# Memory attention begins its first query slices inside the layer norm ahead of it, and the SP queue issues the MoE parameter loads

## The chip, the cores and the metric

One core of a Trainium2 chip runs the whole program once. The metric is device time in microseconds (us) of one execution. 0.3% of it is 5.1 us.

## The reference, cut to what matters

The program is two blocks over 256 tokens of width 1024. The second has two layers, and each runs a mixer, a memory attention and a mixture of experts, with a layer norm after every one:

```python
def layer_norm(x, g, b):
    xf = x.astype(jnp.float32)
    mu = jnp.mean(xf, axis=-1, keepdims=True)
    xc = xf - mu
    var = jnp.mean(xc * xc, axis=-1, keepdims=True)
    y = xc * lax.rsqrt(var + LN_EPS) * g + b
...
def memory_cross_attention(x, mem_k, mem_v, w_q, w_out):
    q = (x @ w_q).reshape(bsz, seq, MEM_HEADS, MEM_HEAD_DIM) * (MEM_HEAD_DIM ** -0.5)
    s = jnp.einsum('bshd,bmhd->bhsm', q, mem_k)
    p = jax.nn.softmax(s, axis=-1)
    o = jnp.einsum('bhsm,bmhd->bshd', p, mem_v).reshape(bsz, seq, MEM_HEADS * MEM_HEAD_DIM)
    return o @ w_out
...
    for i in range(DEPTH):                       # DEPTH is 2
        mix = differential_attention(...) if i == 0 else dsa_sparse_mla(...)
        h = layer_norm(alpha * h + mix, ln_g[i, 0], ln_b[i, 0])
        h = layer_norm(alpha * h + memory_cross_attention(h, ...), ln_g[i, 1], ln_b[i, 1])
        h = layer_norm(alpha * h + hierarchical_moe(h, ...), ln_g[i, 2], ln_b[i, 2])
```

w_q is 1024 by 1024: four heads of 256 columns.

## The kernel before, in words

All matmuls with weights from memory are done in split precision. `split` (L183) makes of a 128x1024 slab a rounded high part `wh` (a cast on ACT, L201, type fp32r) and the rest `wl` (a subtraction, L202, on DVE unless the caller names another engine), and a product is three matmuls: high by high, low by high, high by low. `mm3` (L225 to L227) issues the three for each of the 8 blocks of the contraction; `mm3s` (L240, L241, L243) issues the products with the high part of x first, then the 8 with the low part.

**The end of a mixer.** `diff` (layer 0) and `dsa` (layer 1) end with `nat` (its matmuls are at L225 to L227 with 512 moving columns): the output projection, which leaves two accumulators for each of the two token tiles t = 0, 1 (128 tokens each). Then they call the first layer norm of their layer, called norm 1 here.

**Norm 1** (`layer_norm`, L360 on) runs tile by tile. For each t: DVE adds the mixer to the residual with a row sum (L366, twice 512 columns), makes the mean (L368), ACT squares (L372, twice), DVE subtracts the mean and multiplies by the gain (L375, twice), makes the variance (L376, L377), POOL raises it to the power -1/2 (L378), and DVE scales and shifts (L384, twice). Then PE transposes the tile in 8 blocks (L260), ACT rounds the transpose to `xh` (L263, twice) and DVE takes the rest `xl` (L266, twice). The `xl` of tile 0 are held back (`defer`) until the variance of tile 1 has been sent to POOL.

**Memory attention** (`memattn`, L1432). A queue object (`MoeQueue`) holds the order in which SP loads weight slabs into a ring of buffers (tile name `mw`), and `stream` gives a function that waits for the next slab. Eight q slices of 128 columns (two for a head) are each cast, split and multiplied with all 256 tokens (`proj_T` and `mm3s`: 24 matmuls of 256 columns a slice). After the slices of head 0, PE computes its scores (L1459); slices 2 and 3 (head 1) stand ahead of them. The loop `for n in range(6)` staggers q, softmax (`soft`) and values (`pv`) of the four heads. Then `nat` runs with the output weights, and the second norm of the layer.

**MoE parameters** (`moe_prep`, L1510 on). Nine small loads for the router (`wr` in four pieces, `br` in two, `ust`, `iota`, `first4`) are issued by ACT (L1519 to L1532). `moe_prep` is called between the mixer and `memattn`; ACT has its rows between the casts of the mixer's output weights and the squares of norm 1. They are first read in `route`, at the end of the memory attention's second norm.

The order of instructions on each engine is set by the order of the code and by `tc.issue_after(ins)`, which holds what is written inside it behind the instruction `ins`.

Of the kernel before, what the change touches and what calls it, by code (L numbers as in the profile page):

```python
# [14 lines left out]
AF = mybir.ActivationFunctionType  # L15
ALU = mybir.AluOpType
# [113 lines left out]
class Block:  # L130
# [49 lines left out]
        self.loaded = self.nc.sync.dma_start(v, ap).ins  # L180
        return v

    def split(self, raw, lo_eng=None, pool=None, spare=False):  # L183
        nc = self.nc
        n = int(np.prod(raw.shape[1:]))
        r = []
        if spare == "nrm":
            sp = [self.gp.tile([128, 1024], F32R, tag="nrm", name="sp") for _ in range(2)]
        elif spare:
            sp = self.xp.tile([128, 2, 1024], F32R, tag="xl", name="sp")  # L190
            sp = [sp[:, u] for u in range(2)]
# [12 lines left out]

    def rows(self, ap, lo_eng=None, pool=None):
# [152 lines left out]
    def layer_norm(self, x, mix, li, n, xh=None, xl=None, x32=None, alpha=ALPHA, after=None, fold=1):  # L358
        nc = self.nc
        gb, bb = self.bcast(self.i["ln_g_2"][li, n]), self.bcast(self.i["ln_b_2"][li, n])  # L360
        defer = []
        for t in range(2):
            st = self.small(8, "ln")
            for hf in range(2):
                sl = slice(hf * 512, hf * 512 + 512)
                nc.vector.scalar_tensor_tensor(x[:, t, sl], x[:, t, sl], alpha, mix[t][hf], op0=ALU.mult, op1=ALU.add,  # L366
                                               accum_out=st[:, hf:hf + 1])
            nc.vector.tensor_scalar(st[:, 2:3], st[:, 0:1], st[:, 1:2], -1.0 / D, op0=ALU.add, op1=ALU.mult)  # L368
            sc = self.gp.tile([128, 1024], F32, tag="nrm", name="nrm")
            for hf in range(2):  # L370
                sl = slice(hf * 512, hf * 512 + 512)
                nc.scalar.activation(mix[t][hf], x[:, t, sl], AF.Square, bias=st[:, 2:3], accum_out=st[:, 6 + hf:7 + hf])  # L372
            for hf in range(2):
                sl = slice(hf * 512, hf * 512 + 512)
                nc.vector.scalar_tensor_tensor(sc[:, sl], x[:, t, sl], st[:, 2:3], gb[:, sl], op0=ALU.add, op1=ALU.mult)  # L375
            nc.vector.tensor_scalar(st[:, 3:4], st[:, 6:7], st[:, 7:8], 1.0 / D, op0=ALU.add, op1=ALU.mult)  # L376
            nc.vector.tensor_scalar(st[:, 4:5], st[:, 3:4], 1e-5, None, op0=ALU.add)  # L377
            nc.gpsimd.tensor_tensor(st[:, 5:6], st[:, 4:5], self.mhalf, op=ALU.pow)  # L378
            for f in defer:
                f()  # L380
            for hf in range(2):
                sl = slice(hf * 512, hf * 512 + 512)
                a, b = (v[:, sl].rearrange("p (q k) -> p k q", k=fold) for v in (sc, bb))
                nc.vector.scalar_tensor_tensor(x[:, t, sl].rearrange("p (k q) -> p k q", k=fold), a, st[:, 5:6], b,  # L384
                                               op0=ALU.mult, op1=ALU.add)
# [909 lines left out]
    def diff(self, h):  # L1295
        nc, i, tc = self.nc, self.i, self.tc
# [63 lines left out]
                        nc.vector.scalar_tensor_tensor(o[1][:, j - 1], p[:, 0:256], self.subg, o[0][:, j - 1],  # L1360
                                                       op0=ALU.mult, op1=ALU.subtract)
        acc = self.nat(o, self.rows(wo), lag=4, spare=True)
        x = self.xT()
        self.layer_norm(h, acc, 0, 0, *x)
        return x

    def diff_rope(self, da, t, acc, tag):
        q = self.gp.tile([128, 1024], F32, tag=tag, name="roped")
# [60 lines left out]
            nc.vector.tensor_scalar(on[:, t], po[:, t * 128:t * 128 + 128], s2[:, 4 + t:5 + t], None, op0=ALU.mult)  # L1429
        return on  # L1430

    def memattn(self, h, x, li, after=None):  # L1432
        nc, i, tc = self.nc, self.i, self.tc
        vec, mm = nc.vector, nc.tensor.matmul
        with ExitStack() as es:
            o = self.xT()
            qs, sms = {}, {}
            mq = self.moe_queue
            qcols = mq.stream(2, lambda w, j: self.split(w[:, :, j * 128:j * 128 + 128]))
# [68 lines left out]
    def moe_prep(self, li, es):  # L1508
# [6 lines left out]
            return mc.tile(shape, dt, name=name)  # L1515

        wr = one([128, 8, 20], "wr")
        for c in range(2):
            nc.scalar.dma_start(wr[:, 4 * c:4 * c + 4, 0:4], i["moe_w_group_2"][li, c * 512:c * 512 + 512].rearrange("(p k) g -> p k g", k=4),  # L1519
                                allow_slow_non_contiguous=True)  # L1520
        for c in range(2):
            nc.scalar.dma_start(wr[:, 4 * c:4 * c + 4, 4:20], i["moe_w_expert_2"][li, c * 512:c * 512 + 512].rearrange("(p k) g -> p k g", k=4),
                                allow_slow_non_contiguous=True)
        br = one([128, 20], "br")
        nc.scalar.dma_start(br[:, 0:4], i["moe_b_group_2"][li].partition_broadcast(128))
        nc.scalar.dma_start(br[:, 4:20], i["moe_b_expert_2"][li].partition_broadcast(128))
        ust = one([128, 128], "ust")
        nc.scalar.dma_start(ust, i["ustrict"])
        iota = one([128, 64], "iota")
        nc.scalar.dma_start(iota, i["iota64"])  # L1530
        first4 = one([128, 4], "first4")
        nc.scalar.dma_start(first4, i["first4"])  # L1532
# [60 lines left out]
        r["route"] = route  # L1593
        return r

    def moe(self, h, x32, r, li, last=False):
# [166 lines left out]
    def dsa(self, h, x):  # L1763
# [35 lines left out]
        for t in range(2):  # L1799
# [9 lines left out]
            p = self.ps()  # L1809
# [160 lines left out]
        x = self.xT()  # L1970
        self.layer_norm(h, acc, 1, 0, *x)
        return x


def build(tc, ins, out, start=0, stop=99, hin=None):
    with ExitStack() as es:
# [16 lines left out]
        if stop > 4:  # L1993
# [7 lines left out]
            for li in range(2):  # L2001
                i = b.i
                mem = run((5, 8)[li])
                q = MoeQueue(b.nc, i["xa_w_q_2"][li] if mem else None, i["xa_w_out_2"][li], i["moe_w_gate_2"][li], i["moe_w_up_2"][li], i["moe_w_down_2"][li])
                b.moe_queue = q
                b.extra = 2
                with ExitStack() as ms:
                    early = (4, 6)[li]
                    q.add(ms.enter_context(tc.tile_pool(name="ma", bufs=early, side="right")), early)
                    if run((4, 7)[li]):  # L2010
                        with b.weights(2048, 5 - li, 4):
                            x = (b.dsa(h, x or b.test_x(h)) if li else b.diff(h))
                    for n in (5, 9 - early):
                        q.add(ms.enter_context(tc.tile_pool(name="mw", bufs=n, side="right")), n)
                    r = b.moe_prep(li, ms)
                    q.fetch()
                    if mem:
                        with b.weights(2048, 0, 4):
                            x = b.memattn(h, x or b.test_x(h), li, r["route"] if run((6, 9)[li]) else None)
                    if run((6, 9)[li]):  # L2020
                        if x is None:
                            x = b.test_x32(h)
# [28 lines left out]
```

## Time and profile before

| what | value |
|---|---|
| runs | 1700.69, 1703.74, 1705.14 us; median 1703.74 us |
| the profiled execution | 1703.31 us, span from first to last instruction 1701.2 us, mean granted clock 0.971 |
| busy over the span | PE 1588.7 us (93%), PE weight loads 1157.7, DVE 840.1 (49%), ACT 655.8 (39%), POOL 95.8 (6%) |
| norm 1 of layer 0 | from the last matmul of `nat`, 948.69, to the first scores of head 0, 973.88 us |
| norm 1 of layer 1 | from 1379.84 to 1401.86 us |

How to read it: the page gives for each engine its busy time and the share of the span. A timeline row gives start and length, engine, line, operation, output and inputs by name, shapes, the count of instructions gathered into the row, and in brackets the idle time of the engine before it with what released it. PEld is the weight load of a matmul, which runs beside the matmul before. Rows of PE and PEld say f32 for fp32r too. A length is from start to the modelled end, and ends overlap the next start, so distances are taken from start to start. PEclk is the granted clock of TensorE as a share of full speed.

### The profile page before, as it was taken

The numbers are of one execution on the slowest core, as the hardware profiler recorded it, in microseconds if no ns is written. First come the engines' busy times: TensorE is split into PE (matmuls) and PEld (weight loads), VectorE is DVE, ScalarE is ACT, GpSimd is POOL, SyncE is SP. The second block draws the span as 40 slices with busy tenths as digits, with TensorE's granted clock in tenths as the row PEclk, the third lists the DMA queues.
The fourth block names the chain that finished last, engine by engine and source line by source line (L and its number), as shares of the span: only waits on it lengthen the run. The fifth ranks groups of instructions, "written<-read, shape, count | busy, mean of one in ns | idle before, by whom it ended". The sixth has DMA issues, their size and how long they took to land. (4 is left out here: it accounts for less than half of the span.)

```text
span 1701.2 us, 24789 instructions
## 1 busy us (share of the span) xinstructions
PE 1588.7 (93%) x9871; PEld 1157.7 (68%) x9871; DVE 840.1 (49%) x1831; ACT 655.8 (39%) x1228; POOL 95.8 (6%) x98
## 2 busy tenths in 40 slices
PE   7899999989999999999999798999878989899996
PEld 6777999968767669999788785443327778544342
DVE  3566666475666347665558644111227964511113
ACT  5675555322344236554467432101016744210111
POOL 3610000001100000000101000000000000000000
PEclk9999999989899999999999899999999999999998
DMA  9333755233223448552661846999949257699993
GB/s 345 128 118 115 232 176 173 59 100 112 88 76 104 125 160 263 196 175 98 235 235 42 336 182 230 416 415 416 375 174 327 95 215 284 239 416 414 416 393 125
DMA packets 169771, 375.31 MB, mean 221 GB/s; under 512 B 17188, under 2 KB 106028, under 8 KB 155052
## 3 DMA queue, kind: packets, MB, share of 16 engines
q1 hardware_dynamic: 159696, 363.40, 58.6%
q10 hardware_dynamic: 9948, 10.19, 1.9%
q8 instruction: 82, 1.34, 0.3%
q14 instruction: 45, 0.37, 0.1%
HBM read 372.52 MB, written 1.05 MB: 220 GB/s over the span
## 5 line engine op out<-in xcount | busy, mean ns | idle before, releaser
L202 DVE TENSOR_TENSOR wl<-w,wh 128x1024 fp32r<-128x1024 f32 (+1 forms) x205 | 245.9, 1208 | 178.4 <-ACT wh L201 177.9
L201 ACT CAST wh<-w 128x1024 fp32r<-128x1024 f32 (+1 forms) x221 | 226.8, 1038 | 209.9 <-PE mm L226 125.6
L1669 PE MATMUL mm<-mw,xg 128*64 128x512 f32 x1024 | 231.4, 594 | 0.0
L225 PE MATMUL mm<-xh,wh 128*128 128x256 f32 x800 | 227.2, 284 | 0.4 <-ACT wh L201 0.4
L227 PE MATMUL mm<-xh,wl 128*128 128x256 f32 x800 | 227.4, 284 | 0.0
L226 PE MATMUL mm<-xl,wh 128*128 128x256 f32 x800 | 227.2, 284 | 0.0
L1669 PEld LDWEIGHTS mm<-mw,xg 128*64 128x64 f32 x1024 | 77.6, 137 | 140.6 <-issue 139.8
L225 PEld LDWEIGHTS mm<-xh,wh 128*128 128x128 f32 x800 | 152.4, 190 | 2.5 <-ACT wh L201 0.7
L226 PEld LDWEIGHTS mm<-xl,wh 128*128 128x128 f32 x800 | 151.7, 190 | 2.0
L227 PEld LDWEIGHTS mm<-xh,wl 128*128 128x128 f32 x800 | 151.9, 190 | 0.0
L1711 PE MATMUL mm<-mw,hT 128*64 128x512 f32 x512 | 116.5, 599 | 2.2 <-issue 2.2
L225 PE MATMUL acc<-wh,xh 128*128 128x512 f32 x284 | 113.4, 405 | 1.8 <-ACT xh L263 1.2
L226 PE MATMUL acc<-wl,xh 128*128 128x512 f32 x284 | 114.2, 403 | 0.1
L227 PE MATMUL acc<-wh,xl 128*128 128x512 f32 x284 | 113.5, 401 | 0.0
L1716 ACT ACTIVATE Y<-mm,cs 128x512 fp32r<-128x512 f32 x32 | 22.0, 687 | 166.8 <-PE mm L1711 166.8
L1711 PEld LDWEIGHTS mm<-mw,hT 128*64 128x64 f32 x512 | 39.2, 138 | 69.0 <-issue 67.9
L1675 DVE TENSOR_TENSOR hid<-hid,mm 128x512 f32<-128x512 f32 x16 | 11.0, 688 | 147.2 <-PE mm L1669 147.2
L1717 DVE SCALAR_TENSOR_TENSOR Y<-mm,cs,Y 128x512 fp32r<-128x512 f32 x32 | 24.0, 751 | 117.7 <-ACT Y L1716 115.9
L227 PE MATMUL acc<-wh,fl 128*128 128x512 f32 x176 | 69.8, 396 | 0.0
L225 PE MATMUL acc<-wh,fh 128*128 128x512 f32 x176 | 69.5, 395 | 0.0
L226 PE MATMUL acc<-wl,fh 128*128 128x512 f32 x176 | 69.3, 394 | 0.0
L225 PEld LDWEIGHTS acc<-wh,xh 128*128 128x128 f32 x284 | 53.6, 189 | 14.9 <-ACT xh L263 1.6
(522 smaller groups left out, 2797.5 us busy)
## 6 DMA issues: line engine op xcount, KB each, us to landing
mw<-in_moe_w_down_dram SPq DMA_DIRECT2D x62, 1024.0 KB, 15.6
mw<-in_moe_w_gate_dram SPq DMA_DIRECT2D x58, 1024.0 KB, 8.8
mw<-in_moe_w_up_dram SPq DMA_DIRECT2D x56, 1024.0 KB, 19.9
w<-in_ffn_w_gate_dram SPq DMA_DIRECT2D x22, 1024.0 KB, 6.5
w<-in_ffn_w_up_dram SPq DMA_DIRECT2D x22, 1024.0 KB, 5.4
w<-in_ffn_w_down_dram SPq DMA_DIRECT2D x22, 1024.0 KB, 5.0
w<-in_attn_w_qkv_dram SPq DMA_DIRECT2D x12, 1024.0 KB, 16.2
w<-in_rwkv_w_rkv_dram SPq DMA_DIRECT2D x24, 512.0 KB, 3.7
```

The lines of the kernel that those rows point to most:

```text
L201: nc.scalar.copy(r[0], raw)
L202: (lo_eng or nc.vector).tensor_tensor(r[1], raw, r[0], op=ALU.subtract)
L225: mm(out, lhs[0], rhs[0], start=start, stop=False)
L226: mm(out, lhs[0], rhs[1], start=False, stop=False)
L227: mm(out, lhs[1], rhs[0], start=False, stop=stop)
L1669: mm(ps[64 * e:64 * e + 64], xg[:, k, q % 2 * 128 + e * 64:q % 2 * 128 + e * 64 + 64], mq.slab(w[2 * (k // 4) + e], k % 4), start=k == 0, ...
L1675: tt(hid, hid, gu[1], op=ALU.mult)
L1711: mm(pd[hf][64 * e:64 * e + 64], hT[:, k, 64 * e:64 * e + 64], b, start=k == 0, stop=k == 3)
L1716: act.activation(y[0], pd[hf], AF.Copy, scale=cs)
L1717: vec.scalar_tensor_tensor(y[1], pd[hf], cs, y[0], op0=ALU.mult, op1=ALU.subtract)
```

## The change

`diff` and `dsa` return the accumulators, and `memattn` calls norm 1 itself with `after=started`, which runs after the transposes of each tile. The first four q slices (heads 0 and 1) are multiplied in halves of 128 tokens: after the transposes of tile 0 the products of its `xh` with `wh` and `wl` of all four slices (64 matmuls of 128 columns), after those of tile 1 the rest. They gather in two accumulators, from which `q_of` copies. The low part of slice 0 is made by DVE, of slices 1 to 3 by POOL. Squares, sums and subtractions are ordered by `issue_after`. The nine parameter loads become the function `load`, which `memattn` calls at n = 2, and SP issues them.

```diff
-    def split(self, raw, lo_eng=None, pool=None, spare=False):
+    def split(self, raw, lo_eng=None, pool=None, spare=False, later=None):
...
-            (lo_eng or nc.vector).tensor_tensor(r[1], raw, r[0], op=ALU.subtract)
+            low = lambda: (lo_eng or nc.vector).tensor_tensor(r[1], raw, r[0], op=ALU.subtract)
+            if later is None:
+                low()
+            else:
+                later.append(low)
...
 def layer_norm(...)
-                nc.vector.scalar_tensor_tensor(x[:, t, sl], x[:, t, sl], alpha, mix[t][hf], op0=ALU.mult, op1=ALU.add,
-                                               accum_out=st[:, hf:hf + 1])
+                with self.tc.issue_after(shift) if t else ExitStack():
+                    nc.vector.scalar_tensor_tensor(x[:, t, sl], x[:, t, sl], alpha, mix[t][hf], op0=ALU.mult, op1=ALU.add,
+                                                   accum_out=st[:, hf:hf + 1])
...
-                nc.scalar.activation(mix[t][hf], x[:, t, sl], AF.Square, ...)
+                self.square = nc.scalar.activation(mix[t][hf], x[:, t, sl], AF.Square, ...).ins
...
-            nc.gpsimd.tensor_tensor(st[:, 5:6], st[:, 4:5], self.mhalf, op=ALU.pow)
+            self.pow = nc.gpsimd.tensor_tensor(st[:, 5:6], st[:, 4:5], self.mhalf, op=ALU.pow).ins
...
-                nc.vector.scalar_tensor_tensor(x[:, t, sl]..., a, st[:, 5:6], b, op0=ALU.mult, op1=ALU.add)
+                shift = nc.vector.scalar_tensor_tensor(x[:, t, sl]..., a, st[:, 5:6], b, op0=ALU.mult, op1=ALU.add).ins
...
 # end of diff and of dsa
-        x = self.xT()
-        self.layer_norm(h, acc, 0, 0, *x)
-        return x
+        return acc
...
-    def memattn(self, h, x, li, after=None):
+    def memattn(self, h, mix, x, li, params, after=None):
...
             def q_of(hd):
                 q = half("nrm", hd % 2)
-                self.proj_T(x, qcols, 2 * hd, 2, q)
+                if hd < 2 and mix:
+                    nc.scalar.copy(q, first[hd].rearrange("p (a n) -> p a n", a=2))
+                else:
+                    self.proj_T(x, qcols, 2 * hd, 2, q)
                 return q
+
+            def part(t, lo):
+                for j in range(4):
+                    out = first[j // 2][:, j % 2 * 256 + t * 128:j % 2 * 256 + t * 128 + 128]
+                    xs = [a[:, :, t * 128:t * 128 + 128] for a in x]
+                    for k in range(8):
+                        if lo:
+                            mm(out, wq[j][0][:, k], xs[1][:, k], start=False, stop=t == 1 and j % 2 == 1 and k == 7)
+                        else:
+                            mm(out, wq[j][0][:, k], xs[0][:, k], start=t == 0 and j % 2 == 0 and k == 0, stop=False)
+                            mm(out, wq[j][1][:, k], xs[0][:, k], start=False, stop=False)
+
+            def started(t):
+                if t == 0:
+                    with tc.issue_after(self.square):
+                        wq.extend(qcols(j, nc.gpsimd, None, False, lows) for j in (2, 3))
+                    with tc.issue_after(self.pow):
+                        for low in lows:
+                            low()
+                    first.extend(self.ps() for _ in range(2))
+                    part(0, False)
+                else:
+                    part(0, True)
+                    part(1, False)
+                    part(1, True)
+
+            if mix:
+                self.early, first, lows = 4, [], []
+                wq = [qcols(0), qcols(1, nc.gpsimd)]
+                self.layer_norm(h, mix, li, 0, *x, after=started)
...
+                if n == 2:
+                    params()
...
 # moe_prep: the nine nc.scalar.dma_start calls go, and
+        def load():
+            for u, n, name in ((0, 4, "group"), (4, 16, "expert")):
+                for c in range(2):
+                    nc.sync.dma_start(wr[:, 4 * c:4 * c + 4, u:u + n], ...)
+                nc.sync.dma_start(br[:, u:u + n], i["moe_b_%s_2" % name][li].partition_broadcast(128))
+            for t, name in ((ust, "ustrict"), (iota, "iota64"), (first4, "first4")):
+                nc.sync.dma_start(t, i[name])
```

Where the instructions stand. On PE, in norm 1 of layer 0, before (`c_ident` is the identity of the transposes, `acc` the accumulators of `nat`): the transposes of both tiles are one row, and the slices stand behind it.

```order
L227 MATMUL acc<-wh,xl 128x512
L260 MATMUL mm<-c_ident,h 128x128 x16
L240 MATMUL mm<-xh,wh 128x256
L241 MATMUL mm<-xh,wl 128x256
L240 MATMUL mm<-xh,wh 128x256
```

The same place in the change, at the transposes of tile 1 (the pairs L1470, L1471 ahead of them are the last of 32, those behind the first of 32):

```order
L1470 MATMUL mm<-xh,wh 128x128
L1471 MATMUL mm<-xh,wl 128x128
L264 MATMUL mm<-c_ident,h 128x128 x8
L1468 MATMUL mm<-xl,wh 128x128 x32
L1470 MATMUL mm<-xh,wh 128x128
L1471 MATMUL mm<-xh,wl 128x128
```

The 64 matmuls of tile 0 stand between the two sets of transposes, and the whole pieces for tile 1 behind; PE takes them in this order.

On ACT, in norm 1 of layer 1, before (`w` is a slab of the mixer's output weights, `mw` a q slice):

```order
L201 CAST wh<-w 128x1024 x3
L1519 DMA wr<-in_moe_w_group_dram 128x4x4 x2
L1522 DMA wr<-in_moe_w_expert_dram 128x4x16 x2
L1525 DMA br<-in_moe_b_group_dram 128x4
L1526 DMA br<-in_moe_b_expert_dram 128x16
L372 ACTIVATE acc,ln<-h,ln 128x512 x2
L1528 DMA ust<-in_ustrict_dram 128x128
L1530 DMA iota<-in_iota_dram 128x64
L1532 DMA first_14057<-in_first_dram 128x4
L201 CAST wh<-mw 128x1024
L263 CAST xh<-mm 128x4x128 x2
L372 ACTIVATE acc,ln<-h,ln 128x512 x2
```

and in the change:

```order
L201 CAST wh<-w 128x1024 x3
L377 ACTIVATE acc,ln<-h,ln 128x512 x2
L201 CAST wh<-mw 128x1024 x2
L267 CAST xh<-mm 128x4x128 x2
L201 CAST wh<-mw 128x1024 x2
L377 ACTIVATE acc,ln<-h,ln 128x512 x2
L267 CAST xh<-mm 128x4x128 x2
```

The loads are gone from ACT, and four casts of q slices stand ahead of the squares of tile 1, where one stood.

On POOL, the same norm, before:

```order
L1534 MEMSET ones 128x128
L378 TENSOR_TENSOR ln<-ln,mhalf 128x1 x4
```

and in the change:

```order
L1574 MEMSET ones 128x128
L384 TENSOR_TENSOR ln<-ln,mhalf 128x1
L202 TENSOR_TENSOR wl<-mw,wh 128x1024 x3
L384 TENSOR_TENSOR ln<-ln,mhalf 128x1 x3
```

Three low parts have come between the power of tile 0 and that of tile 1. In layer 0 the row of `wl` of slice 1 stands ahead of the power of tile 0, and two between the powers.

## Rows read from the trace of the kernel before

**Rows 1.** The page: busy time of each engine.
```profile
PE 1588.7 (93%) x9871; PEld 1157.7 (68%) x9871; DVE 840.1 (49%) x1831; ACT 655.8 (39%) x1228; POOL 95.8 (6%) x98
```

**Rows 2.** Timeline of PE, layer 0, norm 1 and the first four slices.
```profile
951.56 1.23 PE L260 MATMUL mm<-c_ident,h 128*128 128x128 f32 x8 [2.47 <-DVE h L384]
958.95 1.94 PE L260 MATMUL mm<-c_ident,h 128*128 128x128 f32 x8 [6.16 <-DVE h L384]
960.71 0.58 PE L240 MATMUL mm<-xh,wh 128*128 128x256 f32 x1
...
964.28 1.12 PE L243 MATMUL mm<-xl,wh 128*128 128x256 f32 x8
...
973.88 1.89 PE L1459 MATMUL mm<-mk,mem 128*128 128x256 f32 x8
```

**Rows 3.** Timeline of PE, layer 1, the same place.
```profile
1380.38 1.29 PE L260 MATMUL mm<-c_ident,h 128*128 128x128 f32 x8
1387.96 1.94 PE L260 MATMUL mm<-c_ident,h 128*128 128x128 f32 x8 [6.29 <-DVE h L384]
...
1401.86 1.89 PE L1459 MATMUL mm<-mk,mem 128*128 128x256 f32 x8
```

**Rows 4.** Windows: busy (count) of PE, PEld, DVE, ACT, POOL; PEclk, DMA share, GB/s.
```profile
959.00:964.00 5.00, 5.00 (x23) 4.78 (x24) 3.36 (x5) 3.66 (x5) 0.00 (x0) 0.50 1.01 421
...
975.00:1050.00 75.00, 68.34 (x380) 55.70 (x380) 40.43 (x103) 29.74 (x61) 1.10 (x2) 0.95 0.48 173
1050.00:1215.00 165.00, 162.19 (x800) 71.56 (x798) 25.32 (x48) 18.22 (x32) 0.00 (x0) 1.00 1.01 412
```

**Rows 5.** Timeline of ACT, layer 0: the first square of norm 1.
```profile
948.02 0.69 ACT L372 ACTIVATE acc<-h,ln 128x512 f32<-128x512 f32 x1 [7.56 <-issue]
```

**Rows 6.** Timeline of ACT, layer 1, norm 1.
```profile
1376.78 0.69 ACT L372 ACTIVATE acc<-h,ln 128x512 f32<-128x512 f32 x1 [5.11 <-DMA wr<-in_moe_w_group_dram]
...
1380.27 1.04 ACT L201 CAST wh<-mw 128x1024 fp32r<-128x1024 f32 x1 [1.97 <-PE acc L227]
1381.22 1.06 ACT L263 CAST xh<-mm 128x512 fp32r<-128x512 f32 x2
1382.39 0.69 ACT L372 ACTIVATE acc<-h,ln 128x512 f32<-128x512 f32 x1
```

**Rows 7.** Timeline of DVE, norm 1: two rows of layer 0, one of layer 1.
```profile
944.58 1.42 DVE L375 SCALAR_TENSOR_TENSOR nrm<-h,ln,gb 128x512 f32<-128x512 f32 x2
...
950.66 1.42 DVE L384 SCALAR_TENSOR_TENSOR h<-nrm,ln,gb 128x512 f32<-128x512 f32 x2 [0.68 <-POOL ln L378]
...
1387.06 1.41 DVE L384 SCALAR_TENSOR_TENSOR h<-nrm,ln,gb 128x512 f32<-128x512 f32 x2 [0.74 <-POOL ln L378]
```

**Rows 8.** The low part of a slab: DVE's group on the page, POOL's timeline, first block.
```profile
L202 DVE TENSOR_TENSOR wl<-w,wh 128x1024 fp32r<-128x1024 f32 (+1 forms) x205 | 245.9, 1208 | 178.4 <-ACT wh L201 177.9
...
29.26 16.71 POOL L202 TENSOR_TENSOR wl<-w,wh 128x1024 fp32r<-128x1024 f32 x7 [1.54 <-ACT wh L201]
```

**Rows 9.** PE with 128-column weights: loads in the timeline, their group, two neighbours.
```profile
1059.95 0.53 PEld L1644 LDWEIGHTS mm<-C,sel 128*128 128x128 f32 x4
...
L1644 PEld LDWEIGHTS mm<-C,sel 128*128 128x128 f32 x64 | 8.4, 191 | 0.0
...
1320.18 0.38 PE L1876 MATMUL mm<-kiz,qiT 128*128 128x128 f32 x2
1320.40 0.60 PE L1877 MATMUL mm<-kiz,qiT 128*128 128x256 f32 x2
```

**Rows 10.** Timeline of SP's queue around norm 1 of both layers.
```profile
951.29 15.06 SPq L91 DMA_DIRECT2D mw<-in_moe_w_up_dram  x4
970.53 0.38 SPq L95 DMA_DIRECT2D mw<-in_moe_w_down_dram  x1
...
1305.89 28.91 SPq L180 DMA_DIRECT2D w<-in_b_w_out_dram  x4
1380.31 0.88 SPq L95 DMA_DIRECT2D mw<-in_xa_w_out_dram  x2
```

More of the change, by code (lines that the diff above doesn't have):

```diff
@@ L371, in layer_norm @@
                 sl = slice(hf * 512, hf * 512 + 512)
-                nc.scalar.activation(mix[t][hf], x[:, t, sl], AF.Square, bias=st[:, 2:3], accum_out=st[:, 6 + hf:7 + hf])
+                self.square = nc.scalar.activation(mix[t][hf], x[:, t, sl], AF.Square, bias=st[:, 2:3],
+                                                   accum_out=st[:, 6 + hf:7 + hf]).ins
             for hf in range(2):
@@ L383, in layer_norm @@
                 a, b = (v[:, sl].rearrange("p (q k) -> p k q", k=fold) for v in (sc, bb))
-                nc.vector.scalar_tensor_tensor(x[:, t, sl].rearrange("p (k q) -> p k q", k=fold), a, st[:, 5:6], b,
-                                               op0=ALU.mult, op1=ALU.add)
+                shift = nc.vector.scalar_tensor_tensor(x[:, t, sl].rearrange("p (k q) -> p k q", k=fold), a, st[:, 5:6], b,
+                                                       op0=ALU.mult, op1=ALU.add).ins
             if xh is not None or x32 is not None:
@@ L1435, in memattn @@
         with ExitStack() as es:
+            x = self.xT() if mix else x or self.test_x(h)
             o = self.xT()
@@ L1438, in memattn @@
             mq = self.moe_queue
-            qcols = mq.stream(2, lambda w, j: self.split(w[:, :, j * 128:j * 128 + 128]))
+            qcols = mq.stream(2, lambda w, j, *a: self.split(w[:, :, j * 128:j * 128 + 128], *a))
             worows = mq.stream(2, lambda w, k, *a: self.split(mq.slab(w, k), None, None, *a))
@@ L1517, in moe_prep @@
         wr = one([128, 8, 20], "wr")
[L1518 to L1523, printed above, removed]
         br = one([128, 20], "br")
-        nc.scalar.dma_start(br[:, 0:4], i["moe_b_group_2"][li].partition_broadcast(128))
-        nc.scalar.dma_start(br[:, 4:20], i["moe_b_expert_2"][li].partition_broadcast(128))
         ust = one([128, 128], "ust")
-        nc.scalar.dma_start(ust, i["ustrict"])
         iota = one([128, 64], "iota")
-        nc.scalar.dma_start(iota, i["iota64"])
         first4 = one([128, 4], "first4")
-        nc.scalar.dma_start(first4, i["first4"])
+        def load():
+            for u, n, name in ((0, 4, "group"), (4, 16, "expert")):
+                for c in range(2):
+                    nc.sync.dma_start(wr[:, 4 * c:4 * c + 4, u:u + n],
+                                      i["moe_w_%s_2" % name][li, c * 512:c * 512 + 512].rearrange("(p k) g -> p k g", k=4),
+                                      allow_slow_non_contiguous=True)
+                nc.sync.dma_start(br[:, u:u + n], i["moe_b_%s_2" % name][li].partition_broadcast(128))
+            for t, name in ((ust, "ustrict"), (iota, "iota64"), (first4, "first4")):
+                nc.sync.dma_start(t, i[name])
         ones = one([128, 128], "ones")
@@ L1591, in choose @@
                 tt(Co, Co, C, op=ALU.mult)
-        r["route"] = route
+        r["route"], r["load"] = route, load
         return r
@@ L1969, in dsa @@
         es.close()
-        x = self.xT()
-        self.layer_norm(h, acc, 1, 0, *x)
-        return x
+        return acc
 def build(tc, ins, out, start=0, stop=99, hin=None):
@@ L2009, in build @@
                     q.add(ms.enter_context(tc.tile_pool(name="ma", bufs=early, side="right")), early)
+                    mix = None
                     if run((4, 7)[li]):
                         with b.weights(2048, 5 - li, 4):
-                            x = (b.dsa(h, x or b.test_x(h)) if li else b.diff(h))
+                            mix = (b.dsa(h, x or b.test_x(h)) if li else b.diff(h))
                     for n in (5, 9 - early):
@@ L2018, in build @@
                         with b.weights(2048, 0, 4):
-                            x = b.memattn(h, x or b.test_x(h), li, r["route"] if run((6, 9)[li]) else None)
+                            x = b.memattn(h, mix, x, li, r["load"], r["route"] if run((6, 9)[li]) else None)
                     if run((6, 9)[li]):
                         if x is None:
+                            r["load"]()
                             x = b.test_x32(h)
```

## The prediction

> **What bounds the kernel now.** I began with the page [rows 1]: PE is busy for 93% of the span, and the other engines for half of it or less. That is an average. What a change in norm 1 is worth is read from that norm, so I went to PE's timeline there. In layer 0 [rows 2] PE is free after the mixer's projection at 951.56 - 2.47 = 949.09, waits 2.47 us for the normed tile 0, transposes it, waits 6.16 us for tile 1, transposes it, and only then multiplies q: 960.71 to 973.88. In layer 1 [rows 3] it waits nothing for tile 0 (the transposes at 1380.38 follow the projection at once) and 6.29 us for tile 1. These three waits are what an earlier start on q can fill. The windows [rows 4] show one cost more: from 959 to 964 the granted clock is 0.50, that is 1.2 GHz. PE had done little but eight transposes before it fell. In layer 0 the first 16 matmuls of q take 964.28 - 960.71 = 3.57 us (0.223 each), and the 80 behind them 973.88 - 964.28 = 9.60 us, 0.120 each [rows 2]. At that pitch the 16 would take 1.9, so the low clock costs 1.65 us.
>
> Then I asked who makes PE wait. In layer 0 the squares of tile 0 start at 948.02 after 7.56 us of idle ACT [rows 5], while DVE was past the mean at 944.58 [rows 7]: ACT is late by some 3.4 us, and ACT's rows there are the parameter loads. In layer 1 the squares wait 5.11 us for a parameter load [rows 6], but it costs nothing, as PE is not free before 1380.38 anyway.
>
> **The pitch of the new matmuls** decides most. The change replaces 96 matmuls of 256 columns by 192 of 128 in each layer. With 128-column weights no fp32r matmul of under 256 columns stands in this trace, so I bound the pitch by neighbours. Four weight loads of 128 columns for matmuls of only two columns take 0.53 us, one load alone 0.191 [rows 9]: (0.53 - 0.19) / 3 = 0.113 from start to start, though there is nearly nothing to stream. Two f32 records of 128 columns with such weights take 1320.40 - 1320.18 = 0.22, 0.110 each [rows 9]. So a load that can't hide behind its predecessor's stream sets about 0.112 us, and that is the value I take, nearest in weights and shape. The lower end is half of 0.120, 0.060, if only streamed columns counted; the upper end for a likely case is 0.120, as if halving the columns saved nothing; the farthest is 0.22, both f32 records for one product.
>
> A matmul's cost thus hardly falls when its columns are halved: 192 x 0.112 = 21.5 us in place of 96 x 0.120 = 11.5, 10 us more PE time in each layer. The question is how much of it lies in the waits.
>
> The Trainium skill (TensorE: Matmul & The Clock Gate, Back-to-back issue gap) gives about 81 ns for each load-and-matmul pair of 128 columns in a sustained stream. No run here shows such a stream; by 0.081 the sum below would be an estimate of -5.9 us, or 1698.
>
> **Layer 0, step by step.** The parameter loads leave ACT, and DVE makes slice 0's low part (1.2 us [rows 8]) ahead of the sums, so the mean comes at 944.5 + 1.2 = 945.7 and the squares start then, 2.3 us earlier than 948.02. ACT's two casts of 1.04 us [rows 6] fit before, in the idle time since 940.46. From first square to shift took 950.66 - 948.02 = 2.64, from shift to transposes 951.56 - 950.66 = 0.90 [rows 2, 5, 7]; so the transposes of tile 0 start at 949.25, and the 64 matmuls with the first `xh` 1.3 later (at the low clock it was 960.71 - 958.95 = 1.76 [rows 2]; 1.3 is my choice for the high one): 950.55 to 957.7. Slices 2 and 3 need POOL's low parts, 16.71 / 7 = 2.39 us each [rows 8], which start after the power (948.35): 950.7 and 953.1, in time for their turns at 954.1 and 955.9. Tile 1 is hidden: its sums stand behind the two shifts of tile 0 (948.35 + 1.42 [rows 7], the sums about as long), so its squares start near 951.9, behind the `xh` casts, and its transposes could start 2.64 + 0.90 later, at 955.5; they start at 957.7. With 1.2 for them and 128 x 0.112 = 14.3 the q of four slices ends at 973.2, against 973.88: **-0.7 us**. All that was won (2.3, the wait of 6.16 and the clock) pays for the doubled loads.
>
> **Layer 1.** Nothing is won at tile 0: its transposes start at 1380.38 as before, and the first cast waits for the projection's last matmul, 1380.27 [rows 6]. Then ACT has two casts, the two `xh`, two casts more: 1380.27 + 2.0 + 1.1 + 1.9 = 1385.2 before the squares of tile 1, which started at 1382.39. POOL is later still: its three low parts stand ahead of tile 1's power and can start only with slice 1's cast, 1382.3, so they end at 1382.3 + 7.2 = 1389.5, and the power of 0.6 lets the shift begin at 1390.1, 3.0 after 1387.06 [rows 7]. PE meanwhile does the 64 matmuls of tile 0, but the last 16 wait for the third low part: 1389.5 + 16 x 0.112 = 1391.3. The transposes of tile 1 stand behind them (1.2), then 14.3: 1406.8 against 1401.86 [rows 3]: **+5.0 us**.
>
> **The rest.** Nine loads on SP: in layer 0 they stand behind the up weights, whose issue ends at 951.29 + 15.06 = 966.35, and the next load goes at 970.53; in layer 1 SP is idle from 1334.8 to 1380.31 [rows 10]. On ACT they took no more than the 7.56 us of [rows 5], so in layer 0 they fill that gap of 4.2 and may push the down weights back by up to 3.4 us. What covers it is that the DMA queues work at 0.48 until 1050 [rows 4], limited by free buffers; the router reads the parameters long after. Cost taken: nothing; without the cover 3.4 us. The two copies from the accumulators take the place of two that ACT made before. What follows slice 3 keeps its order, and the MoE loads, which fill DMA from 1050 on (1.01 [rows 4]), go as buffers come free, so I let the shift pass whole to the end.
>
> **Sum:** -0.7 + 5.0 = +4.3 us against the profiled 1703.31, 1707.6; that run lay 0.4 under the median, so I say **1708**. The 336 matmuls that end on the path (192 and 16 + 128) make 0.336 us for each ns of pitch: at 0.120 the sum is +7.0.
>
> **Rivals.**
> - *Loads hide better than the neighbours show.* With 0.060, layer 0 ends its q by the shift of tile 1: 955.5 + 1.2 + 7.7 = 964.4, -9.5; layer 1 is held by POOL: 1389.5 + 1.0, transposes from 1391.0, 1399.9, -2.0. In all -11.5, **1692**; halfway (0.085) about -4.6, 1699. For it speaks that loads run beside streams; against it both rows of [rows 9]. The figure of the Trainium skill (TensorE: Matmul & The Clock Gate) lies in here. Chance 0.25.
> - *POOL beside a busy DVE is slower.* Its 2.39 us comes from the first block. In layer 1 three low parts stand on the path in a row: every 0.1 us on the length of one costs 0.3. From 2.63 each the change is slower than 0.3% (5.1 us, about what a measurement can tell); at 3.1 it gives +6.4, **1710**. Chance 0.13.
> - *The clock stays at half after the norm.* Matmuls that are mostly loads may not hold it. If the 32 low products of each layer ran at 0.223, that is 3.6 us twice: +11.5, **1715**. Against it: the long waits that came before the fall in [rows 4] are filled. Chance 0.07.
> - *Narrow fp32r runs like f32*, 0.22 each: layer 0 950.55 + 14.1 + 1.2 + 28.2 = 994.0, +20; layer 1 from 1383.4 (the low part of slice 0) to 1426.9, +25; **1749**. Chance 0.06.
> - *The loads on ACT were not what held the squares* (their releaser reads "issue" in [rows 5]): the 2.3 us of layer 0 are not won, +6.6, **1710**. Chance 0.04.
> - *A MoE stage bound by DMA swallows the shift*: no change, 1703. Chance 0.04, and against it the buffers above.
>
> **How the numbers follow.** My own case has 0.41: with a pitch of 0.110 to 0.120 it gives +3.6 to +7.0; 0.32 of it lie within 0.3%, 0.07 above, and 0.02 below, should something be won at tile 0 of layer 1 too. Same: 0.32, 0.02 of the first rival and the 0.04 of the last make 0.38. Faster: the other 0.23 of the first rival and 0.02 make 0.25. Slower: 0.07 + 0.13 + 0.07 + 0.06 + 0.04 = 0.37. The range leaves out the f32 case, half of the clock case and the lower half of the first rival (0.06 + 0.03 + 0.11): 1695 to 1714.
>
> **What would show it.** Right: starts of the 128-column matmuls 0.110 to 0.115 apart at clock 1.0; in layer 1 the power of tile 1 near 1389.5 behind three low parts on POOL, and the first scores near 1406.8, in layer 0 near 973.2; ACT's first square near 945.7. Wrong: a pitch under 0.09; a low part of over 2.6 us on POOL; PEclk at 0.5 in these windows; SP's down weights late with PE waiting for them.

## The result, and the profile after

The change is slower. Its median is 1728.59 us (four runs, 1726.95 to 1730.81) against 1704.44 us of the kernel before (four runs); the ratio is 1.0144, with a 95% interval of 1.0120 to 1.0168. The forecast was 1708 us with a range of 1695 to 1714, so the time lies outside. The profiled execution took 1730.04 us (span 1728.3), 26.7 us more than the one of before; 2.5 of these were lost ahead of norm 1 of layer 0 (PE is free at 953.99 - 2.41 = 951.58, before at 949.09 [rows 2]), in code that the change does not touch. In the profiles of the experiments that place lies between 947.5 and 950.8 us. So everything below is counted from PE's start on norm 1.

PE's timeline in layer 0, from the transposes of tile 0 to the scores of head 0:

```profile
953.99 0.63 PE L264 MATMUL mm<-c_ident,h 128*128 128x128 f32 x4 [2.41 <-DVE h L390]
956.65 1.11 PE L264 MATMUL mm<-c_ident,h 128*128 128x128 f32 x4 [2.03 <-DVE h L390]
957.42 0.46 PE L1470 MATMUL mm<-xh,wh 128*128 128x128 f32 x1
...
971.11 1.93 PE L264 MATMUL mm<-c_ident,h 128*128 128x128 f32 x8
972.69 4.09 PE L1468 MATMUL mm<-xl,wh 128*128 128x128 f32 x32
...
983.77 3.74 PE L1468 MATMUL mm<-xl,wh 128*128 128x128 f32 x32
987.34 1.94 PE L1497 MATMUL mm<-mk,mem 128*128 128x256 f32 x8
```

and in layer 1, the same place:

```profile
1395.33 1.04 PE L264 MATMUL mm<-c_ident,h 128*128 128x128 f32 x8
1398.11 0.33 PE L1470 MATMUL mm<-xh,wh 128*128 128x128 f32 x1 [1.74 <-ACT xh L267]
...
1410.86 1.93 PE L264 MATMUL mm<-c_ident,h 128*128 128x128 f32 x8
1412.44 4.37 PE L1468 MATMUL mm<-xl,wh 128*128 128x128 f32 x32
...
1423.79 3.74 PE L1468 MATMUL mm<-xl,wh 128*128 128x128 f32 x32
1427.37 1.94 PE L1497 MATMUL mm<-mk,mem 128*128 128x256 f32 x8
```

In layer 0 the scores come 987.34 - 951.58 = 35.8 us after PE was free, before 24.8 [rows 2]; in layer 1 they come 32.0 us after the transposes of tile 0, before 21.5 [rows 3]. That is +11.0 and +10.6, nearly the whole loss. The 64 narrow matmuls of tile 0 take 971.11 - 957.42 = 13.7 us, 0.214 each, and 12.75 us in layer 1. The last 32 of layer 0 take 987.34 - 983.77 = 3.57 us, 0.112 each. Windows over these stretches (busy time and count of PE, PEld, DVE, ACT, POOL; PEclk, DMA share, GB/s):

```profile
957.00:972.00 15.00, 15.00 (x73) 15.00 (x72) 5.14 (x13) 2.11 (x5) 0.57 (x1) 0.50 1.02 401
975.00:987.00 12.00, 12.00 (x109) 12.00 (x109) 1.01 (x1) 2.09 (x3) 0.00 (x0) 1.00 0.02 3
1400.00:1411.00 11.00, 11.00 (x53) 10.92 (x53) 4.16 (x7) 1.85 (x5) 6.35 (x4) 0.50 1.02 422
1415.00:1427.00 12.00, 12.00 (x110) 12.00 (x109) 1.03 (x1) 2.12 (x3) 0.00 (x0) 1.00 0.62 258
```

The same matmuls, back to back in all four windows, run at the lower clock (1.2 GHz) in the first of each layer and at the higher one in the second. In layer 0 PE had been idle for 2.41 and 2.03 us with four transposes between; in layer 1 the 64 began at 0.112 and fell to 0.214 after 1400, with the 1.74 us of idle time shortly before.

The second thing to see is DVE in layer 0, beside POOL:

```profile
947.05 0.68 DVE L371 SCALAR_TENSOR_TENSOR h<-h,acc 128x512 f32<-128x512 f32 x1
948.03 1.98 DVE L381 SCALAR_TENSOR_TENSOR nrm<-h,ln,gb 128x512 f32<-128x512 f32 x2
951.01 5.59 DVE L390 SCALAR_TENSOR_TENSOR h<-nrm,ln,gb 128x512 f32<-128x512 f32 x2 [0.68 <-POOL ln L384]
961.45 1.41 DVE L390 SCALAR_TENSOR_TENSOR h<-nrm,ln,gb 128x512 f32<-128x512 f32 x2 [0.68 <-POOL ln L384]
```
```profile
946.30 2.50 POOL L202 TENSOR_TENSOR wl<-mw,wh 128x1024 fp32r<-128x1024 f32 x1 [1.84 <-ACT wh L201]
950.93 5.12 POOL L202 TENSOR_TENSOR wl<-mw,wh 128x1024 fp32r<-128x1024 f32 x2
...
1397.65 8.19 POOL L202 TENSOR_TENSOR wl<-mw,wh 128x1024 fp32r<-128x1024 f32 x3 [3.99 <-ACT wh L201]
```

The two shifts of tile 0 (L390) take 5.59 us where they took 1.42 [rows 7]: they run from 951.01 to 956.60, beside POOL's two low parts (950.93 to 956.05). Those of tile 1, with POOL free, take 1.41. The sum of L371, which runs inside POOL's first low part, keeps its 0.68. L381 and L390 read two operands from SBUF, L371 one of them from the accumulators. In layer 1 POOL's three low parts take 8.19 us, where at 2.39 each [rows 8] they would take 7.2, so POOL seems to be held in turn.

The nine loads are on SP. In layer 0 one of them took 9.26 us to issue, but SP was through with all nine at 974.50, 14 us before its next load:

```profile
960.21 9.26 SPq L1569 DMA_DIRECT2D br<-in_moe_b_group_dram  x1
...
974.07 0.43 SPq L1571 DMA_DIRECT2D first<-in_first_dram  x1
988.68 2.75 SPq L95 DMA_DIRECT2D mw<-in_moe_w_down_dram  x2
```

### The profile page after: what moved, and what is told of

It is laid out like the page before. It is cut to its first block, busy times and chain, and to the rows that moved or that the text cites. A ratio compares the mean times of both kernels' runs of the same rounds, so it can differ in the third digit from the quotient of the medians.

```text
span 1728.3 us, 25161 instructions
## 1 busy us (share of the span) xinstructions
PE 1623.7 (94%) x10063; PEld 1192.4 (69%) x10063; DVE 840.3 (49%) x1825; ACT 655.1 (38%) x1228; POOL 111.6 (6%) x104
## 5 line engine op out<-in xcount | busy, mean ns | idle before, releaser
L229 PE MATMUL mm<-xh,wh 128*128 128x256 f32 x752 | 213.9, 284 | 0.4 <-ACT wh L201 0.4
L231 PE MATMUL mm<-xh,wl 128*128 128x256 f32 x752 | 213.9, 284 | 0.0
L230 PE MATMUL mm<-xl,wh 128*128 128x256 f32 x752 | 213.4, 284 | 0.0
L229 PEld LDWEIGHTS mm<-xh,wh 128*128 128x128 f32 x752 | 143.3, 190 | 2.5 <-ACT wh L201 0.7
L230 PEld LDWEIGHTS mm<-xl,wh 128*128 128x128 f32 x752 | 142.9, 190 | 2.0
L231 PEld LDWEIGHTS mm<-xh,wl 128*128 128x128 f32 x752 | 142.7, 190 | 0.0
```

The lines of the kernel that those rows point to most:

```text
L229: mm(out, lhs[0], rhs[0], start=start, stop=False)
L230: mm(out, lhs[0], rhs[1], start=False, stop=False)
L231: mm(out, lhs[1], rhs[0], start=False, stop=stop)
```

## The experiments

My theory after this result: three things add up. The halves double the weight loads (the forecast's own sum); TensorE's clock falls just ahead of the narrow matmuls and stays low under them; DVE is held while POOL subtracts. Rivals: that one of these is all, or that a fourth is there.

**PE kept busy.** An f32 matmul of 256 columns, its result thrown away, fills PE's waits:

```diff
+    def busy(self, out, n):
+        for _ in range(n):
+            self.nc.tensor.matmul(out[:, 0:256], self.mk[:, 0, 0:128], self.mk[:, 0], start=True, stop=True)
...
+                self.busy(self.ps(), (5, 2)[li])
                 self.layer_norm(h, mix, li, 0, *x, after=started)
...
                     first.extend(self.ps() for _ in range(2))
+                    self.busy(first[0], (0, 4)[li])
```

> The change with extra f32 matmuls of 256 columns (0.43 us each at the high clock, results thrown away) in PE's waits: ahead of the transposes of tile 0 five in layer 0 and two in layer 1, and four more in layer 1 ahead of the first narrow matmul. Theory 'clock' (the 64 matmuls of tile 0 run at 0.214 from start to start in place of 0.112 because TensorE was idle just before, and it costs about 7 us in layer 0 and 6 in layer 1): PEclk stays at 1.0 in layer 1, its 64 matmuls come at 0.112, layer 1 gains 5 to 6 us; layer 0 gains up to 7, or less if the 2.3 us wait between the two halves of the transposes still lets the clock fall. Total 1716 to 1723 us. Rival 'narrow matmuls cannot hold the clock': it falls again within the 64, gain under 2 us, 1727 to 1729. Rival 'DVE behind POOL is most of the loss': no gain, 1728.

Measured: ratio 1.0145 (1.0117 to 1.0173), six runs from 1727.47 to 1744.38. By the time alone, no gain, and the theory of the clock seems to fall. The profile, which is of one of the two longest runs (1744.08 us, mean granted clock 0.958; the four runs under 1734 have 0.966 and no profile), says otherwise. Its windows in layer 1 (PE's busy time, PEclk, DMA share, GB/s) and three rows of its timeline:

```profile
1400.00:1406.00 6.00, 4.89 (x42) 1.00 1.04 427
1408.00:1437.00 29.00, 29.00 (x139) 0.50 0.50 209
```
```profile
1403.67 0.33 PE L1475 MATMUL mm<-xh,wl 128*128 128x128 f32 x1 [0.79 <-POOL wl L202]
1406.00 0.33 PE L1475 MATMUL mm<-xh,wl 128*128 128x128 f32 x1 [0.32 <-POOL wl L202]
1431.02 7.03 PE L1472 MATMUL mm<-xl,wh 128*128 128x128 f32 x32
```

The clock did hold at first, so PE was now fast enough to wait for POOL's low parts (0.79 us, and 0.32 more for the next), and right behind the second of these waits it fell: from 1406.4 on the pitch is 0.21. Then it did not come back at all: 29 us of 128-column matmuls back to back (the transposes of tile 1 among them), up to the scores, ran at the low clock. In layer 0 the wait between the two halves of the transposes (DVE behind POOL) was still there, 2.31 us more went by for the second half of `xh`, which ACT made behind the squares of tile 1, and the clock fell as in the change. The edit cured neither layer, and the run shows what a fall can cost. By itself it also fits the rival that narrow matmuls cannot hold the clock; the third experiment decides that.

**Low parts on DVE.**

```diff
-                        wq.extend(qcols(j, nc.gpsimd, None, False, lows) for j in (2, 3))
+                        wq.extend(qcols(j, None, None, False, lows) for j in (2, 3))
...
-                wq = [qcols(0), qcols(1, nc.gpsimd)]
+                wq = [qcols(0), qcols(1, None, None, False, lows)]
```

> The change with the low parts of slices 1 to 3 made by DVE in place of POOL. Theory 'DVE is held while POOL subtracts' (in layer 0 the two shifts of tile 0 took 5.6 us in place of 1.4): the shift is back at 1.4 us, the 64 matmuls of layer 0 start about 3 us earlier after the end of the projection (one more low part of 1.2 us stands ahead of the mean), and if PE's wait is then too short for the clock to fall, another 6 us are won: 1719 to 1726. In layer 1 the power of tile 1 comes some 3 us earlier, which is won only if PE is ahead of it. Rival 'clock alone': layer 0 gains under 1 us, 1727 to 1729.

Measured: ratio 1.0107 (1.0052 to 1.0162); the four runs are 1713.33, 1714.93, 1729.04 and 1730.65, and the profile is of 1714.93. Its shift in layer 0, and windows of norm 1 of both layers:

```profile
949.87 1.41 DVE L390 SCALAR_TENSOR_TENSOR h<-nrm,ln,gb 128x512 f32<-128x512 f32 x2 [0.68 <-POOL ln L384]
```
```profile
950.00:975.00 25.00, 24.12 (x210) 23.50 (x211) 11.93 (x21) 7.27 (x13) 0.56 (x1) 1.00 0.88 338
1384.00:1396.00 12.00, 12.00 (x59) 12.00 (x58) 4.81 (x8) 1.86 (x5) 0.56 (x1) 0.50 1.02 421
```

With POOL out of the way the shift is back at 1.41 us, PE's waits in layer 0 are short and its clock stays high: the scores come 24.9 us after PE was free, 10.8 less than in the change. Layer 1, where PE still idles 1.74 us ahead of the narrow matmuls, runs at the low clock as in the change. That two of the runs are 15 us longer fits a clock that also fell in layer 0, or stayed low longer (their mean granted clocks are 0.963 and 0.960, those of the two short runs 0.972 and 0.969), but only one run has a profile. What it shows holds for the short runs; the median of the four, 1721.99 us, lies between the two groups and says little.

**Both edits.**

> Both of the edits before: low parts on DVE and PE kept busy. If clock and DVE are the two causes, both norms run at PEclk 1.0 throughout, and what is left is my forecast's own sum, the doubled weight loads: within 5 us of the kernel before, 1703 to 1709. If a third cause is there, it stays above 1712.

Measured: 1709.86 us (ten runs, 1706.39 to 1712.26), ratio 1.0018 (1.0003 to 1.0032). Windows over norm 1 and the narrow matmuls of both layers, and the first scores:

```profile
952.00:976.00 24.00, 23.76 (x211) 1.00 0.84 321
1384.00:1408.00 24.00, 24.00 (x211) 1.00 0.99 402
```
```profile
975.75 1.51 PE L1503 MATMUL mm<-mk,mem 128*128 128x256 f32 x6
...
1408.61 1.94 PE L1503 MATMUL mm<-mk,mem 128*128 128x256 f32 x8
```

Clock and waiting are mended, and about 21 us of the loss are back (ratios 1.0144 and 1.0018, each against runs of the kernel before made beside it). From the second experiment this kernel differs only by the thrown-away matmuls, and in layer 1 the clock is 1.00 in place of 0.50: with PE's waits filled the clock no longer falls. At the high clock the narrow matmuls hold it for 24 us in both layers, so the rival that they cannot is out; so is the traffic of the DMA queues as the cause (share 0.99 at PEclk 1.00 here, 1.02 at 0.50 in the change). What is left is near the forecast's own sum: counted from the projection's end (950.14 and 1383.07) the scores come 0.8 us later than before in layer 0 (forecast -0.7) and 3.9 in layer 1 (forecast +5.0). No fourth cause of more than a few us is needed.

**Wide matmuls in the middle**, to see what brings the clock back. The change, with

```diff
+                        if not lo and not t and j == 1 and not k:
+                            self.busy(self.ps(), 5)
                         if lo:
```

> The change with five f32 matmuls of 256 columns (10 records, thrown away) put in the middle of the 64 narrow ones, after those of slice 0, in both layers. Question: what brings the clock back. Theory 'matmuls that are mostly weight loads do not raise a low clock, streamed columns do': the pitch of the narrow matmuls falls from 0.214 to 0.112 right behind the wide ones or during them, so the remaining 48 take 5.4 us in place of 10.3, the wide ones cost about 2 to 4: 1724 to 1729, and PEclk is 1.0 about 8 us earlier in layer 0. Rival 'the clock comes back some time after it fell, whatever PE does': the narrow ones behind the wide ones still come at 0.214 until about 16 us after the fall, 1732 to 1736.

Measured: 1718.98 us (four runs, 1717.29 to 1721.55), ratio 1.0081 (1.0056 to 1.0105): adding ten records of work makes the change about 10 us faster. Timeline in layer 0, and windows ahead of and behind these rows and in layer 1:

```profile
956.78 3.64 PE L239 MATMUL mm<-mk 128*128 128x256 f32 x10
960.07 0.41 PE L1476 MATMUL mm<-xh,wh 128*128 128x128 f32 x1
960.32 0.27 PE L1477 MATMUL mm<-xh,wl 128*128 128x128 f32 x1
960.43 0.28 PE L1476 MATMUL mm<-xh,wh 128*128 128x128 f32 x1
```
```profile
954.00:958.00 4.00, 4.00 (x17) 0.50 1.02 420
961.00:980.00 19.00, 19.00 (x173) 1.00 0.45 154
1394.00:1413.00 19.00, 19.00 (x173) 1.00 0.96 395
```

Right behind the wide ones the narrow come 0.11 apart and keep the high clock for 19 us, in both layers. The gain is larger than I expected, as the clock rose while the wide ones still ran and held through all that follows. In windows of 1 us PEclk passes from 0.50 to 1.00 near 959.3 in layer 0, some 2.5 us after the first wide one, so it was low for about 7 us, in the change for about 17: the rival of a fixed time is out.

**The loads alone.** The kernel before, with only the nine loads moved (the function `load` of the change, called at n = 2).

> The kernel before with only the nine MoE parameter loads moved from ACT's queue to SP's, in the place that the change gives them. Theory 'the loads on ACT held the squares of layer 0': the first square starts about 2.5 us earlier against the end of the projection, PE's wait for tile 0 falls from 2.5 us to near nothing, the scores come 2 us earlier, layer 1 stays: ratio 0.998 to 0.999 (1.5 to 3 us faster). Rival 'they held nothing': ratio 1.000, squares where they were.

Measured: 1699.52 us (ten runs, 1698.28 to 1701.88), ratio 0.9966 (0.9954 to 0.9978): 5.8 us faster, twice the upper end of what I had said. Rows of its timeline: ACT's first square of layer 0, and PE's transposes and scores in both layers.

```profile
945.13 0.69 ACT L372 ACTIVATE acc<-h,ln 128x512 f32<-128x512 f32 x1 [2.76 <-DVE ln L368]
```
```profile
948.67 1.23 PE L260 MATMUL mm<-c_ident,h 128*128 128x128 f32 x8
954.92 1.94 PE L260 MATMUL mm<-c_ident,h 128*128 128x128 f32 x8 [5.03 <-DVE h L384]
969.74 1.89 PE L1459 MATMUL mm<-mk,mem 128*128 128x256 f32 x8
...
1376.77 1.03 PE L260 MATMUL mm<-c_ident,h 128*128 128x128 f32 x8
1397.54 1.89 PE L1459 MATMUL mm<-mk,mem 128*128 128x256 f32 x8
```

The square now waits for the mean on DVE, not for ACT's queue. PE's wait of 2.47 us for tile 0 [rows 2] is gone, and from tile 0 to tile 1 it takes 954.92 - 948.67 = 6.25 us in place of 7.39: the first q slice can be cast and split ahead of the norm, so its low part stands no more between DVE's sums. Layer 0 gains 3.7 us so (scores 21.1 after PE was free), layer 1 0.7 (20.8 from its transposes). The other part of the 5.8 lies within the interval (2 us each way).

**The loads, and PE kept busy in the order of before**: twelve of the f32 matmuls behind the transposes of tile 0.

> The kernel before with the loads on SP and, in both layers, twelve f32 matmuls of 256 columns (5.2 us, results thrown away) between the transposes of tile 0 and those of tile 1. Theory 'PE's idle time ahead of the slices lowers the clock and the first slice pays for it': PEclk 1.0 from norm 1 on, the transposes of tile 1 take 1.1 to 1.3 us in place of 1.94, no q matmul at 0.22; gains 2.3 us in layer 0 and 1.3 in layer 1, with the loads 5 to 6 us: ratio 0.9965 to 0.998. Rival 'the clock falls anyway': as the run with only the loads moved.

Measured: 1699.43 us, ratio 0.9963 (0.9951 to 0.9976). In the profile PEclk is 1.00 in both norms and the scores come 1.9 and 1.0 us earlier than with the loads alone (expected 2.3 and 1.3), but the whole is not faster. In its profiled run the stretch from the scores of layer 1 to the end is 2.8 us longer (1699.2 - 1396.63 against 1697.3 - 1397.54). Whether that is given back there each time, I did not settle.

**Halves that keep 256 columns.** The tokens of one tile become the stationary operand, a slab of w moves, and q is turned afterwards; low parts on DVE, PE kept busy:

```diff
+            def part(t, hd, lo):
+                out = first[t][:, hd * 256:hd * 256 + 256]
+                ts = slice(t * 128, t * 128 + 128)
+                for k in range(8):
+                    w = wq[2 * hd + k // 4]
+                    if lo:
+                        mm(out, x[1][:, k, ts], w[0][:, k % 4], start=False, stop=...)
+                    else:
+                        mm(out, x[0][:, k, ts], w[0][:, k % 4], start=..., stop=False)
+                        mm(out, x[0][:, k, ts], w[1][:, k % 4], start=False, stop=False)
```

> A form of the change in which the halves keep 256 moving columns: the transposed x of one tile (128 tokens) is the stationary operand and a slab of 256 q columns moves, 96 matmuls for the four slices in place of 192, and q of heads 0 and 1 is turned by eight transposes afterwards; low parts on DVE, PE kept busy in its waits, slices 4 and 5 ahead of the scores. Theory 'the loss of the halves at full clock is the doubled weight loads': q matmuls 0.120 apart, of which half lie in the wait for tile 1, so the four slices end about 18 to 20 us after the projection's end in layer 0 (24.8 before) and 20 to 22 in layer 1 (21.6 before): 3 to 7 us faster than before, ratio 0.996 to 0.998. Rival 'the waits for low parts and turns eat it': ratio 0.999 to 1.003.

> The form with the tokens as stationary operand again, but with the loop over heads as in the change: the scores of head 0 stand ahead of slices 4 and 5, those of head 1 behind them. Theory 'the four slices did end early, and the softmax of heads 0 and 1 behind slice 5 gave it back': the scores of head 0 come about 18 us after the projection's end in layer 0 (21.1 with only the loads moved) and 18 to 19 in layer 1 (20.6 to 20.8), and 4 us are won over that kernel: ratio to the kernel before 0.993 to 0.996. Rival 'turning q and waiting for the copies eats what the 256 columns save': ratio 0.996 to 0.999.

Measured: 1700.24 us, ratio 0.9971 (0.9960 to 0.9982), and 1700.85 us, ratio 0.9978 (0.9965 to 0.9991). Against the narrow halves with the same mended waits (1.0018) that is 7 to 8 us better, but it is no better than moving the loads alone. The first ratio lies where its theory put it, but the loads, which this form contains, give as much by themselves. In the second the scores of head 0 come 21.1 us after PE was free in layer 0, as with the loads alone, and 21.9 in layer 1 (expected 18 to 19):

```profile
970.23 1.99 PE L1520 MATMUL mm<-mk,mem 128*128 128x256 f32 x8
```

The turns wait for copies of q (0.56 and 0.78 us in layer 0), and half of head 1's products stand ahead of the scores. The rival of the second expectation holds.

**The halves undone**, everything else of the change kept:

```diff
-                    part(0, False)
                 else:
-                    part(0, True)
-                    part(1, False)
-                    part(1, True)
+                    for j in range(4):
+                        self.mm3s(first[j // 2][:, j % 2 * 256:j % 2 * 256 + 256], wq[j], x, 8, j < 1)
```

> The change with the halves undone and the rest kept (loads on SP, low parts of slices 1 to 3 on POOL, early casts): the four slices are multiplied with all 256 tokens in 96 matmuls of 256 columns behind the transposes of tile 1. Theory 'the narrow matmuls, at either clock, are most of the loss, and DVE held by POOL a smaller part': the shifts of tile 0 in layer 0 still take some 5.6 us, PE waits longer for tile 1 than before (1 to 2 us in layer 0, 3 to 4 in layer 1), but the 96 come at 0.120 after a short cold start, so the scores come 25 to 27 us after the projection's end in both layers (35.8 and 31.9 in the change): 1710 to 1715 us. Rival 'what stands on POOL and ACT ahead of tile 1 is most of the loss': over 1720.

Measured: 1711.45 us (ten runs, 1708.86 to 1715.58), ratio 1.0042 (1.0026 to 1.0057). Its shift of tile 0, PE's wait for tile 1 in layer 1, and the first scores of both layers:

```profile
946.92 5.59 DVE L390 SCALAR_TENSOR_TENSOR h<-nrm,ln,gb 128x512 f32<-128x512 f32 x2 [0.68 <-POOL ln L384]
```
```profile
972.76 1.89 PE L1495 MATMUL mm<-mk,mem 128*128 128x256 f32 x8
...
1391.34 1.94 PE L264 MATMUL mm<-c_ident,h 128*128 128x128 f32 x8 [10.83 <-DVE h L390]
...
1406.03 1.89 PE L1495 MATMUL mm<-mk,mem 128*128 128x256 f32 x8
```

DVE is held as in the change, and PE waits 10.8 us for tile 1 of layer 1 in place of 6.3 [rows 3]. The scores come 25.3 and 26.6 us after PE was free (35.8 and 32.0 in the change). Without the halves 17 of the change's 24 us are gone. The loads alone stand at a ratio of 0.9966, so the low parts on POOL and the casts ahead of the squares cost some 13 us by themselves, the low clock behind the longer waits included. Against the loads alone, then, the halves with mended waits cost about 9 us (third experiment), what stands on POOL and ACT about 13, and the whole change about 30. The 8 us that neither gives alone fit narrow matmuls running at a clock that the waits have lowered; no run takes them apart.

## Why the prediction was wrong, point by point

- **The pitch at the high clock was right**: 0.112 us taken, 0.112 measured. The Trainium skill (TensorE: Matmul & The Clock Gate, Back-to-back issue gap) has about 81 ns for such a stream; here the measurement decides. (By that figure the forecast's own sum comes to -6.1 us, not to the -5.9 that stands there.)
- **The step that failed is "the 64 matmuls with the first `xh` 1.3 later ...: 950.55 to 957.7"**, and its counterpart in layer 1. It priced all 64 at the high clock; they took 0.214 each. In layer 0 that is 13.7 - 7.2 = 6.5 us, in layer 1 the 64 end 4.6 us later than forecast (15.5 us after the transposes, forecast 10.9); the transposes of tile 1 and the first low products, still at the low clock, add 0.7 and 1.0. About 13 of the 17 us that the sum missed (21.6 measured in the two norms, 4.3 forecast) lie in these matmuls. Of the 4.6 in layer 1 some 1.4 would have been there at the high clock too, as POOL's third low part, for which the last 16 wait, ended only at 1405.84 (an estimate: 1405.84 + 16 x 0.112 is 12.3 us after the transposes); so the clock makes about 11.
- **My rival on the clock had the price in the wrong place.** It let the 32 low products run slow, and its argument against was that the waits are filled. They are filled only behind the wait for tile 0, and [rows 4] already showed the low clock in norm 1, behind PE's waits there. For that, 0.07 was too small a chance.
- **The low parts on POOL were taken as free for DVE.** I weighed POOL's length (2.39 us) and what stands behind it on POOL, not what it does to DVE. The shift of 5.59 us delays the 64 matmuls by 4.4 us in layer 0 (957.42 is 5.8 us after PE was free, forecast 1.5), and it makes the two waits (2.41 and 2.03 us) ahead of the fall of the clock. In the profile of the second experiment, where the shift takes 1.41 us, the clock of layer 0 stays at 1.00. The Trainium skill has the rule (SBUF — State Buffer, Who interferes with whom): a DVE instruction with two SBUF inputs and a GpSimd one that reads SBUF block each other, the later waiting for the other to end. The trace agrees (5.59 against 1.42 us, and L371 with an accumulator operand keeps 0.68), and I had not looked for it.
- **Layer 1's delay on POOL was right in kind**: the power of tile 1 came 10.5 us after the transposes of tile 0 (1405.79 - 1395.33), forecast 9.1. It did not show, because at the low clock PE was later still.
- **The loads were undersized**: 2.3 us forecast in layer 0, 3.7 measured there and 5.8 in all. That SP has room for them held in the change, although one load took 9.26 us to issue.
- **The doubled weight loads cost somewhat more than was said.** With clock and DVE mended the halves stand about 9 us above the kernel with only the loads moved (ratios 1.0018 and 0.9966). The forecast's sum without the 2.3 us that it gave the loads says 6.6. That the whole of it still came out near (0.8 + 3.9 us against 4.3) is partly luck, as the loads gave more than forecast and the halves cost more.

## What to carry to other kernels

Halving the moving columns of a matmul does not halve its cost where the weight load that each one needs sets the pitch (here 0.112 us in place of 0.120), so work pulled into a wait in such halves pays only if nearly all of the first half fits there: here 192 x 0.112 = 21.5 us stood against 11.5, and 10 us of narrow matmuls, about 90 of tile 0's 96, would have had to be hidden before anything was won, while the wait for tile 1 was 6.2 us [rows 2]. Price work that follows a wait of PE at both clock levels, and look in the trace for places where the granted clock already falls. Before giving POOL an elementwise job, see which DVE instructions will run beside it, and how many of their operands lie in SBUF.

The version to keep is the kernel before with the parameter loads on SP, at 0.9966 of its time.

## What was not expected of the hardware

- A low clock outlasted 29 us of back-to-back 128-column matmuls in the first experiment. Where the clock is high, the same matmuls keep it (24 us in the third, 19 in the fourth). In the change it came back 2 to 3 us after the transposes of tile 1 began, in the first experiment's layer 1 the same transposes did not bring it back; why they differ is open.
- Ten wide f32 records, 3.64 us of wasted work, made the change about 10 us faster.
- Two DVE instructions, 1.41 us together, took 5.59 beside POOL instructions that share no data with them, and POOL's own three, 7.2 us at 2.39 each, took 8.19.
